# RMS normalisation of rows on one core: the first store on ScalarE's queue cut to one row, two stores and two loads of the first slot joined

## The chip, the cores and the metric

The kernel runs on one core of one Trainium2 chip. The metric is the device time of one execution in microseconds (us). All engine names are those of the profile: PE is TensorE, DVE is VectorE, ACT is ScalarE, POOL is GpSimd, SP is SyncE, which here only issues DMAs. ACT issues some DMAs too, on a queue of its own.

## The reference

```python
# x: 16 x 1024 x 512, float32; gamma: 512, float32
rms = np.sqrt(np.mean(x ** 2, axis=-1, keepdims=True) + 1e-5)
return (x / rms * gamma).astype(np.float32)
```

Each of the 16384 rows of 512 numbers is divided by its root mean square and multiplied by gamma. In and out are 33.55 MB each, and every byte is moved once.

## The kernel before

**Tiles and slots.** The rows are cut into 4 tiles (0 to 3). A tile has 128 partitions with 32 consecutive rows each, so 8.39 MB; "rows a to b" below means rows a to b of every partition, and in memory these are one run of 2 KB a row per partition. There are three slots (`slots`, line 40) of a tile's size in SBUF. Tiles 0, 1 and 2 live in slots 0, 1 and 2; tile 3 is loaded into slot 0 again, so its load has to wait until tile 0 is stored. Everything is done in place. An unwritten part of slot 2, its rows 23 to 31, serves as scratch for the squares of the groups with a piece of 9 rows (line 91), which is why these rows of tile 2 are loaded by themselves, later.

**Groups.** `groups` (line 76) lists the units of work in order: (tile, first row, rows, pieces, share of POOL). Tile 0 has three groups (rows 0-6, 7-15, 16-31), the others two each (rows 0-15, 16-31). For every group:

- `square_sums` (L96, L97): for each piece ACT squares the rows into PSUM, an SBUF scratch or slot 2, and DVE adds up each row.
- `inverse_rms` (L102, L103): ACT takes the root, DVE the reciprocal.
- `scale_by_pool` (L109, L110): POOL does the last 3, 5 or 7 rows of the group alone, first times 1/rms, then times gamma.
- `scale` (L118): ACT multiplies the other rows by 1/rms, one instruction a row.
- `times_gamma` (L122): DVE multiplies these rows by gamma, which lies in PSUM (PE spread it there at the start).

**Order.** The schedule is manual: each engine runs its instructions in the order of the program text. The loop from line 163 on is software-pipelined: while group k is scaled, the squares and sums of group k+1 are made. On ACT, the first two squares of group k+1 come ahead of the first half of the scaling of group k, and a third square ahead of the second half. So a square that waits for a load holds the scaling of the group before it.

**Transfers.** `load` (L45) goes on SP's queue, `store` (L49) on SP's or ACT's. A DMA instruction waits, on its issuing engine, for the semaphores of what it reads or overwrites; a reader of loaded rows waits for the semaphore of the DMA that brought them, which is full when the whole DMA has landed. SP's list, in order: tile 0 in four loads with gamma in between, tile 1 in two, tile 2 rows 0-22, then store tile 0 rows 8-15, store tile 0 rows 16-31, load tile 2 rows 23-31, load tile 3 rows 0-15, load tile 3 rows 16-31, store tile 1 rows 4-31, store tile 2, store tile 3 in two halves. ACT's list has three stores: tile 0 rows 0-3 (line 173, after the first squares of the group from row 16), tile 0 rows 4-7 (line 179) and tile 1 rows 0-3 (line 181).

Of the kernel before, what the change touches and what calls it, by code (L numbers as in the profile page):

```python
# [9 lines left out]
def kernel(  # L10
# [6 lines left out]
    nc = tc.nc  # L17
# [26 lines left out]
    def load(t, slot, r0, r1):  # L44
        dma = nc.sync.dma_start(out=slots[slot][:, r0:r1], in_=xv[t][:, r0:r1])  # L45
        before_scale.append((slot, r0, r1, dma))

    def store(t, slot, r0, r1, queue=nc.sync):
        dma = queue.dma_start(out=ov[t][:, r0:r1], in_=slots[slot][:, r0:r1])  # L49
        before_scale.append((slot, r0, r1, dma))  # L50
# [38 lines left out]
    def square_sums(ss, t, g, r, m, k):  # L89
        if m == 9:  # L90
            sq = slots[2][:, 23:32, :]
        else:
            home, name, most = ((psum, "sq_psum", 7), (const, "sq_sbuf", 5))[k % 2]
            sq = home.tile([P, most, D], fp32, name=name)
        rows = slots[slot_of[t]][:, g + r : g + r + m, :]
        nc.scalar.activation(out=sq[:, :m], in_=rows, func=AF.Square)  # L96
        nc.vector.tensor_reduce(  # L97
            out=ss[:, r : r + m, 0], in_=sq[:, :m], axis=mybir.AxisListType.X, op=OP.add
        )

    def inverse_rms(ss, n):
        nc.scalar.activation(out=ss[:, :n, 0], in_=ss[:, :n, 0], func=AF.Sqrt, bias=eps_t, scale=1.0 / D)  # L102
        nc.vector.reciprocal(out=ss[:, :n, 0], in_=ss[:, :n, 0])  # L103
        return ss

    def scale_by_pool(rstd, t, g, n, share):
        part = slots[slot_of[t]][:, g + n - share : g + n, :]
        by_row = rstd[:, n - share : n].to_broadcast([P, share, D])
        nc.gpsimd.tensor_tensor(out=part, in0=part, in1=by_row, op=OP.mult)  # L109
        last = nc.gpsimd.tensor_tensor(  # L110
            out=part, in0=part, in1=gamma_b.to_broadcast([P, share, D]), op=OP.mult
        )
        before_scale.append((slot_of[t], g + n - share, g + n, last))

    def scale(rstd, t, g, r0, r1):
        x = slots[slot_of[t]]
        for r in range(r0, r1):
            nc.scalar.activation(out=x[:, g + r, :], in_=x[:, g + r, :], func=AF.Copy, scale=rstd[:, r])  # L118

    def times_gamma(t, g, r0, r1):  # L120
        part = slots[slot_of[t]][:, g + r0 : g + r1, :]
        scaled = nc.vector.tensor_tensor(  # L122
            out=part, in0=part, in1=gamma_psum.to_broadcast([P, r1 - r0, D]), op=OP.mult
        )
        for slot, b0, b1, earlier in before_scale:
            if slot == slot_of[t] and b0 < g + r1 and g + r0 < b1:
                tc.declare_no_dep(scaled.ins, earlier.ins, reason="ScalarE waited for it before it scaled these rows")

    def transfers(t, g):
        if (t, g) == (0, 0):  # L130
            load(1, 1, 16, 32)
            load(2, 2, 0, 23)
        elif (t, g) == (0, 16):
            store(0, 0, 8, 16)
            store(0, 0, 16, 32)
            load(2, 2, 23, 32)
            load(3, 0, 0, 16)
            load(3, 0, 16, 32)
        elif (t, g) == (1, 16):
            store(1, 1, 4, 32)  # L140
        elif (t, g) == (2, 16):
            store(2, 2, 0, 32)
        elif (t, g) == (3, 0):
            store(3, 0, 0, 16)
        elif (t, g) == (3, 16):
            store(3, 0, 16, 32)

    def pieces_of(group):
        t, g, n, pieces, share = group
        ss = stats.tile([P, 16, 1], fp32, name="ss")  # L150
        r = 0
        todo = []
        for k, m in enumerate(pieces):
            todo.append((ss, t, g, r, m, k))
            r += m
        return ss, todo
# [6 lines left out]
    for k, group in enumerate(groups):  # L163
        t, g, n, pieces, share = group
        mine = n - share
        half = (mine + 1) // 2
        ahead = groups[k + 1 :][:1]
        ss, todo = pieces_of(ahead[0]) if ahead else (None, [])
        scale_by_pool(rstd, t, g, n, share)
        for piece in todo[:2]:  # L170
            square_sums(*piece)
        if (t, g) == (0, 7):
            store(0, 0, 0, 4, nc.scalar)
        scale(rstd, t, g, 0, half)
        for piece in todo[2:]:
            square_sums(*piece)
        scale(rstd, t, g, half, mine)
        if (t, g) == (0, 16):
            store(0, 0, 4, 8, nc.scalar)
        elif (t, g) == (2, 0):  # L180
            store(1, 1, 0, 4, nc.scalar)
        times_gamma(t, g, 0, mine)
        transfers(t, g)
        for nxt in ahead:
            rstd = inverse_rms(ss, nxt[2])
# [30 lines left out]
```

## Time and profile before

| what | value |
|---|---|
| median of 3 runs | 161.56 us (161.45 to 161.64) |
| the profiled execution's own time | 161.69 us |
| its span in the trace | 159.8 us |
| DVE busy | 112.0 us (70% of the span), 39 instructions |
| ACT busy | 107.8 us (67%), 108 instructions |
| POOL busy | 106.4 us (67%), 24 instructions |
| PE busy | 2.0 us (1%) |
| SP's queue (q1) | 63.97 MB, 93.5% of 16 DMA engines' span |
| ACT's queue (q10) | 3.15 MB, 4.7% |

Times within the execution are counted from the start of the span. The span is what the trace shows from first to last event; the execution's own time is 1.9 us longer. A landing is the moment at which a DMA's semaphore is full; each of the 16 DMA engines adds its part, and the trace records these 16 completions one by one. The trace also records each packet that a DMA engine moved, with its queue, start, length in bytes and duration; in this kernel a packet is one partition's run of rows, so each DMA of 128 partitions is 8 packets on each of 16 engines. A share of the queues above is the time that its packets took.

### The profile page before, as it was taken

The page shows a single profiled execution, that of the slowest core. Times are in us where ns is not written, and L with a number is a line of the kernel's source. Part 1 is how long each engine was busy: PE and PEld are TensorE (multiplying, and loading weights), DVE is VectorE, ACT ScalarE, POOL GpSimd, SP SyncE. Part 2 cuts the span into 40 slices and gives each one's busy share as a digit, 9 for nine tenths or more (in the row PEclk, how much of TensorE's full clock was granted, in tenths as well). Part 3 has the DMA queues.
Part 4 walks back from the last instruction along what each step waited for, and adds up shares of the span by engine and source line. Part 5 has one row for each costly group of instructions (what it writes and reads, how often), then busy time and mean ns, then how long its engine had stood idle before and what let it go on. Part 6 is the DMA issues. An engine that isn't in the chain of part 4 may idle for free.

```text
span 159.8 us, 273 instructions
## 1 busy us (share of the span) xinstructions
PE 2.0 (1%) x2; PEld 0.5 (0%) x2; DVE 112.0 (70%) x39; ACT 107.8 (67%) x108; POOL 106.4 (67%) x24
## 2 busy tenths in 40 slices
PE   0050000000000000000000000000000000000000
PEld 0010000000000000000000000000000000000000
DVE  0019098899798999999999999999999009800000
ACT  3071966975999999999899999989970990000000
POOL 1000960994999599999999999999999990000000
DMA  5999999999999998998999999999996997999995
GB/s 179 431 427 468 443 418 410 377 449 408 455 476 443 443 410 365 423 500 370 434 468 394 470 445 390 501 459 459 459 476 279 525 476 312 394 468 451 394 435 222
DMA packets 2747, 67.12 MB, mean 420 GB/s; under 512 B 313, under 2 KB 314, under 8 KB 442
## 3 DMA queue, kind: packets, MB, share of 16 engines
q1 hardware_dynamic: 2314, 63.97, 93.5%
q10 hardware_dynamic: 432, 3.15, 4.7%
q14 instruction: 1, 0.01, 0.0%
HBM read 33.56 MB, written 33.55 MB: 420 GB/s over the span
## 4 chain that ended last, share of the span: by engine, by line
DVE 59%; ACT 21%; DMA 4%; issue 1%; ACTq 1%; SPq 0%
DVE ss L97 36%; DVE slot L122 23%; ACT slot L118 8%; ACT slot L96 8%; ACT sq_psum L96 5%; DMA slot<-in_x_dram 4%; DVE ss L103 1%; ACT ss L102 0%; ACTq L211 0%; ACT gamma_b L162 0%; SPq L45 0%; ACTq L49 0%; ACTq L96 0%
## 5 line engine op out<-in xcount | busy, mean ns | idle before, releaser
L109 POOL TENSOR_TENSOR slot<-slot,ss 128x3584 f32<-128x3584 f32 (+2 forms) x9 | 46.9, 5213 | 24.2 <-DVE ss L103 24.2
L110 POOL TENSOR_TENSOR slot<-slot,gamma_b 128x3584 f32<-128x3584 f32 (+2 forms) x9 | 59.2, 6582 | 0.7
L97 DVE TENSOR_REDUCE ss<-sq_psum 128x7 f32<-128x3584 f32 (+1 forms) x13 | 42.2, 3245 | 13.7 <-ACT sq_psum L96 13.7
L118 ACT ACTIVATE slot<-slot,ss 128x512 f32<-128x512 f32 x75 | 47.2, 706 | 4.7 <-DVE ss L103 4.7
L122 DVE TENSOR_TENSOR slot<-slot,gamma_psum 128x4608 f32<-128x4608 f32 (+2 forms) x9 | 41.3, 4589 | 8.7 <-ACT slot L118 8.7
L96 ACT ACTIVATE sq_psum<-slot 128x3584 f32<-128x3584 f32 (+1 forms) x13 | 34.5, 2657 | 6.3 <-DMA slot<-in_x_dram 5.7
L97 DVE TENSOR_REDUCE ss<-slot 128x9 f32<-128x4608 f32 x3 | 14.9, 4954 | 4.4 <-ACT slot L96 4.2
L97 DVE TENSOR_REDUCE ss<-sq_sbuf 128x5 f32<-128x2560 f32 x5 | 14.0, 2800 | 0.0
L96 ACT ACTIVATE slot<-slot 128x4608 f32<-128x4608 f32 x3 | 12.1, 4032 | 0.0
L96 ACT ACTIVATE sq_sbuf<-slot 128x2560 f32<-128x2560 f32 x5 | 11.6, 2324 | 0.3 <-DMA slot<-in_x_dram 0.3
L102 ACT ACTIVATE ss<-ss,eps_t 128x16 f32<-128x16 f32 (+2 forms) x9 | 2.7, 304 | 11.7 <-DVE ss L97 11.7
L103 DVE RECIPROCAL ss<-ss 128x16 f32<-128x16 f32 (+2 forms) x9 | 2.1, 235 | 0.4 <-ACT ss L102 0.4
L66 PE MATMUL gamma_psum<-gamma_row,ones_col 1*128 1x512 f32 x2 | 2.0, 1122 | 8.7 <-DMA gamma_row<-in_gamma_dram 8.7
L72 ACT ACT_TABLE_LOAD x1 | 1.3, 1283 | 1.2 <-PEq L200 1.2
L162 ACT COPY gamma_b<-gamma_psum 128x512 f32<-128x512 f32 x1 | 0.6, 564 | 0.0
L66 PEld LDWEIGHTS gamma_psum<-gamma_row,ones_col 1*128 1x128 f32 x2 | 0.5, 305 | 8.6 <-issue 8.6
L64 POOL MEMSET ones_col<- 1x128 f32 x1 | 0.2, 194 | 0.3 <-POOLq L200 0.3
L200 POOL MEMSET const-float32-0.0<- 128x1 f32 x1 | 0.1, 98 | 0.2 <-issue 0.2
L72 ACT ACTIVATE table<-eps_t 128x1 f32<-128x1 f32 x1 | 0.2, 202 | 0.0
L200 POOL MEMSET const-bfloat16-1.0<- 128x1 bf16 x1 | 0.1, 101 | 0.0
L200 POOL MEMSET const-uint8-127<- 128x1 uint8 x1 | 0.1, 101 | 0.0
L200 POOL MEMSET const-float32-1.0<- 128x1 f32 x1 | 0.1, 98 | 0.0
(1 smaller groups left out, 0.1 us busy)
## 6 DMA issues: line engine op xcount, KB each, us to landing
slot<-in_x_dram SPq DMA_DIRECT2D x5, 4096.0 KB, 25.0
out_dram<-slot SPq DMA_DIRECT2D x3, 4096.0 KB, 20.2
out_dram<-slot SPq DMA_DIRECT2D x1, 7168.0 KB
slot<-in_x_dram SPq DMA_DIRECT2D x1, 5888.0 KB
out_dram<-slot ACTq DMA_DIRECT2D x3, 1024.0 KB
slot<-in_x_dram SPq DMA_DIRECT2D x1, 2304.0 KB, 25.7
slot<-in_x_dram SPq DMA_DIRECT2D x1, 2048.0 KB, 10.0
out_dram<-slot SPq DMA_DIRECT2D x1, 2048.0 KB
```

The costliest lines, as they stand in the source:

```text
L66: nc.tensor.matmul(gamma_psum[:, 0], ones_col, gamma_row, start=True, stop=True)
L72: nc.scalar.activation(out=table, in_=eps_t, func=AF.Sqrt)
L96: nc.scalar.activation(out=sq[:, :m], in_=rows, func=AF.Square)
L97: nc.vector.tensor_reduce(out=ss[:, r : r + m, 0], in_=sq[:, :m], axis=mybir.AxisListType.X, op=OP.add)
L102: nc.scalar.activation(out=ss[:, :n, 0], in_=ss[:, :n, 0], func=AF.Sqrt, bias=eps_t, scale=1.0 / D)
L103: nc.vector.reciprocal(out=ss[:, :n, 0], in_=ss[:, :n, 0])
L109: nc.gpsimd.tensor_tensor(out=part, in0=part, in1=by_row, op=OP.mult)
L110: last = nc.gpsimd.tensor_tensor(out=part, in0=part, in1=gamma_b.to_broadcast([P, share, D]), op=OP.mult)
L118: nc.scalar.activation(out=x[:, g + r, :], in_=x[:, g + r, :], func=AF.Copy, scale=rstd[:, r])
L122: scaled = nc.vector.tensor_tensor(out=part, in0=part, in1=gamma_psum.to_broadcast([P, r1 - r0, D]), op=OP.mult)
L162: nc.scalar.copy(out=gamma_b[:, 0], in_=gamma_psum[:, 0])
L200: nc = _bacc.Bacc("TRN2", target_bir_lowering=False, num_devices=1)
```

## The change

Row 0 of tile 0 goes out alone in the first store on ACT's queue, rows 1 to 7 in the second, where there were 0 to 3 and 4 to 7. Tile 0's rows 8 to 31 are stored by one DMA on SP's queue, at the place in the program where the second of two stood. Tile 3's 32 rows are loaded by one DMA in place of two.

In the instruction lists, SP's has one store and one load fewer; the order on all other engines is what it was. The semaphores of the later DMAs are dealt out anew, since the DMAs of the program take eight of them in turn.

```diff
         elif (t, g) == (0, 16):
-            store(0, 0, 8, 16)
-            store(0, 0, 16, 32)
+            store(0, 0, 8, 32)
             load(2, 2, 23, 32)
-            load(3, 0, 0, 16)
-            load(3, 0, 16, 32)
+            load(3, 0, 0, 32)
...
         if (t, g) == (0, 7):
-            store(0, 0, 0, 4, nc.scalar)
+            store(0, 0, 0, 1, nc.scalar)
         scale(rstd, t, g, 0, half)
...
         if (t, g) == (0, 16):
-            store(0, 0, 4, 8, nc.scalar)
+            store(0, 0, 1, 8, nc.scalar)
```

## Prediction

> **What bounds the kernel now.** I read the page's second part first, then the stretches, the DMA issues and the timelines of SP, ACT and DVE. Two rows of the page, the DMA engines' busy tenths in 40 slices of 4 us and the bytes:
>
> ```profile
> DMA  5999999999999998998999999999996997999995
> HBM read 33.56 MB, written 33.55 MB: 420 GB/s over the span
> ```
>
> No compute engine passes 70%, but the 16 DMA engines are full from the first slice to the last (a packet counts in the slice in which it starts, hence the 6 and 7 late on, where packets are long). The view by stretches gives the rate; the last columns are DMA share and GB/s:
>
> ```profile
> 0.70:1.70 1.00, 0.00 (x0) 0.00 (x0) 0.00 (x0) 0.53 (x1) 0.23 (x2) 1.00 0.00 0
> 1.70:2.00 0.30, 0.00 (x0) 0.00 (x0) 0.00 (x0) 0.30 (x1) 0.00 (x0) 1.00 0.94 109
> ...
> 28.00:32.00 4.00, 0.00 (x0) 0.00 (x0) 3.40 (x1) 4.00 (x2) 4.00 (x1) 1.00 0.95 354
> 32.00:81.30 49.30, 0.00 (x0) 0.00 (x0) 47.53 (x17) 45.13 (x45) 45.13 (x8) 1.00 1.01 436
> ...
> 139.60:149.30 9.70, 0.00 (x0) 0.00 (x0) 0.00 (x0) 0.00 (x0) 0.00 (x0) 1.00 1.00 432
> ```
>
> So some 433 GB/s, with no hole between transfers. The bytes do not change, so the time changes only if the queues run empty. The page's chain of waits names DVE (59%); that chain ends in a store that was issued early enough to queue, so DVE's slack counts, not its share. The issues of SP that set it (start, duration):
>
> ```profile
> 76.33 0.33 SPq L45 DMA_DIRECT2D slot<-in_x_dram  x1
> 111.67 0.34 SPq L49 DMA_DIRECT2D out_dram<-slot  x1
> 139.25 0.33 SPq L49 DMA_DIRECT2D out_dram<-slot  x1
> ```
>
> They are load(3, rows 16-31), store(2, all rows) and the last store, whose landing comes 19.7 us after issue (view of DMA issues), at 158.95. Back from there at 433 GB/s: 4.19 MB is 9.69 us, so store(3, 0-15) lands at 149.3, store(2) at 139.6, store(1, 4-31) at 120.2. **Slack** of the issue before the queue empties: 120.2 - 111.7 = 8.5 us for store(2), 13.9 for store(3, 0-15) (issued 125.65), 10.0 for the last. Packets end about 0.4 us before the landing is recorded (single packet records: 158.0 to 158.6 against 158.95), so the queue of store(1) is dry, as a mean over the engines, at 119.55 unless store(2) stands behind it.
>
> **Part 1: the ACT stores, one row and seven in place of four and four.** Both are issued where they were (27.41 and 40.02), on the same waits by the instruction lists: the first still follows DVE's product of rows 0-3. Bytes are equal, and SP's loads keep the engines full (436 GB/s from 32 on). Packets are one row-run per partition, so 2 and 14 KB in place of 8 and 8. The second must land before tile 3 may be loaded. Before, it took from 40.02 to 59.7 (recorded completions); seven rows in 8 rounds beside SP's 46 KB packets (433 GB/s are 27 an engine) take 8 x (1.74 + 0.53) = 18.2 us after a start near 44, landing near 62, long before 76. Cost 0. One thing is open: 28 to 32, around the first ACT store, moves 354 GB/s where 433 is usual, 0.32 MB or 0.7 us. If that is the price of this store's size, up to -0.7; if more, smaller packets cost, as much again. No other ACT store shows it; I take 0.
>
> **Part 2: store(0, 8-31) in one.** SP issued rows 8-15 at 39.78 and 16-31 at 55.45. Now all wait for DVE's product of rows 16-24 (ends 55.4) and go at 55.45. Ahead of them stands load(2, 0-22), recorded as landing at 61.5: 6 us of cover, some 5 after a start-up of about 1. Same bytes, same place in SP's queue: 0. Only with that cover gone would it cost.
>
> **Part 3: load(3) in one; here the price is.** Its issue waits for store(0, 8-31) to land (76.2, as the rows 16-31 did; load 3 of rows 16-31 went at 76.33) and has load(2, 23-31) ahead of it in the queue until 81.5: no hole. But rows 0-15 were issued at 66.45, landed 25.1 us later, at 91.55, and ACT squared them at once:
>
> ```profile
> 91.61 0.31 ACT L102 ACTIVATE ss<-ss,eps_t 128x16 f32<-128x16 f32 x1 [0.35 <-DVE ss L97]
> 91.82 3.14 ACT L96 ACTIVATE sq_psum<-slot 128x3584 f32<-128x3584 f32 x1
> 94.90 2.32 ACT L96 ACTIVATE sq_sbuf<-slot 128x2560 f32<-128x2560 f32 x1
> 97.13 3.15 ACT L118 ACTIVATE slot<-slot,ss 128x512 f32<-128x512 f32 x5
> 100.37 1.88 ACT L96 ACTIVATE sq_psum<-slot 128x2048 f32<-128x2048 f32 x1
> 102.19 2.54 ACT L118 ACTIVATE slot<-slot,ss 128x512 f32<-128x512 f32 x4
> ```
>
> Now one semaphore covers all 32 rows (in the instruction list the square at 91.82 waits for this DMA, the one of rows 16-31 for none). Behind it on ACT's queue stand the nine row scalings (L118) of tile 2's second half, and DVE's product and store(2) wait for those.
>
> When does it land? Rows 16-31 landed at 103.4 (last recorded completion), after the whole 1.05 MB of the ACT store of tile 1 (issued 86.70). That store's 8 KB packets (0.31 us) go in between SP's, nearly one for one, the first 3.65 us after issue, three of SP's 32 KB packets (1.21 us) later. SP's packets are now 64 KB and take 2.42 us (those of store(2), same size, do), so fewer ACT packets get ahead of the load's eight. It starts at 81.1; packets end at 83.5, 85.9, 88.4, 90.8, 93.2...; ACT's enter at 90.8 or 93.2, and 4 or 3 of 8 are in before the eighth. So 103.4 less 4 or 5 times 0.31: **102.0**. Bounds: all ahead 103.4; none ahead 100.9.
>
> By the Trainium skill (DMA: Bandwidth & Descriptors, Queues, rings and completion order) an engine drains a whole packet of some 9 to 17 descriptors from one row before it switches, so the eight pieces would go together. The trace shows them one by one here; by the page the bound of 103.4 would hold and the time be near 164.6.
>
> From there: ACT starts 0.08 us after a landing (81.53 to 81.61 at tile 2's last rows), so 102.1, not 91.82. DVE's rows of before:
>
> ```profile
> 96.52 3.82 DVE L97 TENSOR_REDUCE ss<-sq_psum 128x7 f32<-128x3584 f32 x1
> 100.26 2.80 DVE L97 TENSOR_REDUCE ss<-sq_sbuf 128x5 f32<-128x2560 f32 x1
> 102.98 2.28 DVE L97 TENSOR_REDUCE ss<-sq_psum 128x4 f32<-128x2048 f32 x1
> 105.18 4.94 DVE L122 TENSOR_TENSOR slot<-slot,gamma_psum 128x4608 f32<-128x4608 f32 x1
> ```
>
> Before, DVE was the later one; now ACT is. ACT by its own starts: 3.1 + 2.2 + 3.2 + 1.8 + 2.5 = 12.8 us to the end of the last scaling (DVE's first reduction, of 7 rows, ends 7.0 after the start, before ACT's third square needs its tile at 8.5), so the product starts at 114.9, ends at 119.85, and store(2) is issued at 119.9 (POOL's part is done at 111.65). A start on an idle queue: first load issued at 0.74, nothing moves until 1.7, 0.94 busy after it, some 1.1 us to the mean first packet. On a busy queue 3.65 (above) was measured. I take 1.1, because the queue is empty: packets from 121.0. **Gap 121.0 - 119.55 = 1.45 us.**
>
> By the Trainium skill (DMA: Bandwidth & Descriptors, Specifications) the first byte on this path takes about 0.6 us; by it the gap would be 0.95. No row here restarts a store on an empty queue.
>
> What is late next: tile 3's halves. DVE is full again, so from product to product 13.69 us as before (105.18 to 118.87), and 15.38 from there to the last product's end: 119.85 + 13.7 + 15.4 = 148.95, issue at 149.0, packets from 150.1. The queue before it empties at 121.0 + 19.4 + 9.7 = 150.1. So the last store is just at the edge: 0 to 0.4, I take 0.15.
>
> **Sum**: 0 + 0 + 1.45 + 0.15 = +1.6 us. The profiled execution took 161.69 (span 159.8, 1.9 around it), so 163.3; it lies 0.13 above the median 161.56, and that gives **163.2 us**.
>
> **Rivals.**
> - *Later landing*: all ACT packets go ahead of the load, 103.4, gap 1.4 larger: 164.6. Against: the one-for-one mix.
> - *Slow restart*: an empty queue needs the 3.65 us of the busy one, so 2.55 more: 165.7. For: it is measured on a store; against: there packets stood ahead.
> - *Not slower, hidden*: the load goes ahead of ACT's packets altogether. Landing at 100.9, store(2) at 118.8, packets at 119.9: gap 0.35, time 161.9; it decides at a landing of 100.85, where 0.3 us is left: just beyond that bound, or at it with a restart quicker by 0.05. For: long packets are favoured; against: ACT's are due three of the load's packets before its end.
> - *Faster*: fewer, larger transfers pay, and the last rows come in time. Of the transfers' borders none shows a hole (432 GB/s over 139.6 to 149.3); only the 0.7 us at 28 to 32 could be won: 160.9 without a gap. The Trainium skill (DMA: Bandwidth & Descriptors, Rules for kernel authors) advises to coalesce into one large transfer, which speaks for this change; the trace shows no cost between queued ones.
> - The change does do what it says: SP's list has one store and one load fewer, the other engines' orders are unchanged.
>
> **Chances.** Forecast (landing 101.6 to 102.4, restart 1.0 to 1.6, edge 0 to 0.4, so +1.0 to +2.6) 0.68; later landing 0.10; slow restart 0.09; hidden or nearly 0.08, of which 0.05 within 0.2% (0.32 us, about what a measurement of this kernel can tell from none); faster 0.05. Faster 0.05, same 0.05, slower 0.90. The range 162.0 to 165.0 holds the forecast, the later landing and part of the nearly hidden.
>
> **What would show it.** The DMA row: a hole near 120 us, and not before. ACT idle from 91.9 to 102, DVE from 96.5 to 105.3. store(2) issued at 119.9 in place of 111.7, the last at 149.0. ACT's second store landing near 62, load(3) issued at 76. If load(3) is issued later, or a hole shows near 60 or 80, parts 1 or 2 are wrong; if the hole is 3 us and more, the restart or the landing is.

## The result, and the profile after

The changed kernel takes 163.79 us (median of 6 runs, 163.24 to 164.93), the kernel before 161.60 (161.45 to 161.71): a ratio of 1.0145, with a 95% interval of 1.0116 to 1.0175. That is 2.2 us more, where 1.6 was forecast. The profiled execution is the longest of the six: 164.93 us, span 163.1. So its profile shows about 1 us more than the median, and the experiments below are needed to say which part of its loss is steady.

The same two rows of the page as before, busy tenths of the DMA engines and bytes:

```profile
DMA  6999899999989998897997989999919959889885
HBM read 33.56 MB, written 33.55 MB: 411 GB/s over the span
```

The bytes are the same, the rate over the span is 411 GB/s in place of 420, and one slice, the thirtieth (118.3 to 122.4 us), holds a 1 where the others hold 5 to 9. Seen closely, in the view by stretches (the last two columns are DMA share and GB/s; a packet counts in the stretch in which it starts):

```profile
116.00:118.00 2.00, 0.00 (x0) 0.00 (x0) 1.80 (x2) 2.00 (x4) 0.00 (x0) 1.00 1.06 459
118.00:120.00 2.00, 0.00 (x0) 0.00 (x0) 2.00 (x1) 2.00 (x1) 0.00 (x0) 1.00 0.27 115
120.00:122.00 2.00, 0.00 (x0) 0.00 (x0) 2.00 (x3) 2.00 (x2) 0.00 (x0) 1.00 0.00 0
122.00:124.00 2.00, 0.00 (x0) 0.00 (x0) 2.00 (x2) 2.00 (x4) 1.87 (x1) 1.00 1.23 524
```

No packet starts between 120 and 122. ACT and DVE are busy there and POOL is idle: the queue waits for computed rows. ACT's timeline names the cause; the bracket is the idle time before an instruction and what ended it:

```profile
92.03 0.29 ACT L102 ACTIVATE ss<-ss,eps_t 128x16 f32<-128x16 f32 x1
104.16 3.16 ACT L96 ACTIVATE sq_psum<-slot 128x3584 f32<-128x3584 f32 x1 [11.84 <-DMA slot<-in_x_dram]
107.26 2.32 ACT L96 ACTIVATE sq_sbuf<-slot 128x2560 f32<-128x2560 f32 x1
109.48 3.17 ACT L118 ACTIVATE slot<-slot,ss 128x512 f32<-128x512 f32 x5
112.56 1.86 ACT L96 ACTIVATE sq_psum<-slot 128x2048 f32<-128x2048 f32 x1
114.36 2.55 ACT L118 ACTIVATE slot<-slot,ss 128x512 f32<-128x512 f32 x4
```

ACT stands 11.84 us before the square of tile 3's first rows, for their load. The scalings of tile 2 (L118, from 109.48) stand behind it, though their rows had landed by 82.4 and DVE had made their 1/rms by 97.3. Then DVE's product, and SP's store of tile 2, which went at 111.67 before; the third line is the last store:

```profile
116.94 4.95 DVE L122 TENSOR_TENSOR slot<-slot,gamma_psum 128x4608 f32<-128x4608 f32 x1 [0.20 <-ACT slot L118]
```

```profile
76.58 0.33 SPq L45 DMA_DIRECT2D slot<-in_x_dram  x1
121.96 0.34 SPq L49 DMA_DIRECT2D out_dram<-slot  x1
151.06 0.33 SPq L49 DMA_DIRECT2D out_dram<-slot  x1
```

By the records of single packets, store(1)'s last packets ended between 119.51 and 121.62, as a mean at 120.2, and store(2)'s first started between 122.80 and 122.95, 0.9 us after the issue. So the engines stood idle for 2.7 us on average. In the kernel before, store(1)'s last packets ended at 119.6 as a mean: another 0.6 us had been lost ahead of the hole.

One thing was not forecast. The load's sixteen completions lie at 101.84 to 102.59 for twelve DMA engines, around the 102.0 of the prediction, and at 103.84 to 104.14 for four. ACT waits for the last.

### The profile page after: what moved, and what is told of

Its sections match the earlier page's. It is cut to its first block, busy times and chain, and to the rows that moved or that the text cites. A ratio compares the mean times of both kernels' runs of the same rounds, so it can differ in the third digit from the quotient of the medians.

```text
span 163.1 us, 270 instructions
## 1 busy us (share of the span) xinstructions
PE 2.0 (1%) x2; PEld 0.5 (0%) x2; DVE 112.6 (69%) x39; ACT 107.7 (66%) x108; POOL 106.3 (65%) x24
## 4 chain that ended last, share of the span: by engine, by line
DMA 34%; DVE 27%; ACT 27%; issue 3%; ACTq 1%; SPq 0%
DMA slot<-in_x_dram 21%; DVE ss L97 14%; DVE slot L122 13%; DMA out_dram<-slot 13%; ACT slot L118 11%; ACT slot L96 7%; ACT sq_psum L96 6%; ACT sq_sbuf L96 1%; ACT ss L102 0%; ACTq L209 0%; ACT gamma_b L160 0%; SPq L45 0%; ACTq L49 0%; DVE ss L103 0%; SPq L49 0%
## 5 line engine op out<-in xcount | busy, mean ns | idle before, releaser
L118 ACT ACTIVATE slot<-slot,ss 128x512 f32<-128x512 f32 x75 | 47.4, 708 | 4.7 <-DVE ss L103 4.7
```

## The experiments

They ran on two chips, each beside runs of the kernel before, whose medians lie at 161.59 to 161.65. The second run of ACT's stores, the two runs that cut its seven rows and the last run are from one chip, all others from another. Theory A is that of the prediction: the load in one lands as a whole, ACT's queue stands, store(2) comes after its queue is dry. The rivals: the new transfer sizes make DMA engines lag (B), or the loss is in parts 1 or 2 (C).

**The load in one, alone.**

```diff
-            load(3, 0, 0, 16)
-            load(3, 0, 16, 32)
+            load(3, 0, 0, 32)
```

> Only tile 3 is loaded in one; the four stores of tile 0 are as before. Theory A (the one load lands as a whole, ACT's square of tile 3's first half waits for it, holds tile 2's scaling, and the queue runs dry near 120 us): all of the loss is here, 163.2 to 163.8 us, store(2) issued near 120 or later. Theory B (the new sizes, 2, 14 and 48 KB packets, make DMA engines lag behind the others, and that is the larger part): less than half of the loss, below 162.6. Theory C (the loss is in parts 1 or 2, the load's price is hidden): 161.6.

Measured: 163.01 us (162.89 to 163.32), ratio 1.0086 (1.0067 to 1.0105), so 1.4 us. Its SP issues of store(2) and of the last store:

```profile
120.01 0.34 SPq L49 DMA_DIRECT2D out_dram<-slot  x1
149.09 0.33 SPq L49 DMA_DIRECT2D out_dram<-slot  x1
```

and its stretches around the hole:

```profile
117.00:118.80 1.80, 0.00 (x0) 0.00 (x0) 1.80 (x1) 1.80 (x2) 0.00 (x0) 1.00 1.18 510
118.80:119.20 0.40, 0.00 (x0) 0.00 (x0) 0.40 (x1) 0.40 (x1) 0.00 (x0) 1.00 0.00 0
119.20:120.60 1.40, 0.00 (x0) 0.00 (x0) 1.40 (x3) 1.40 (x2) 0.43 (x1) 1.00 0.01 0
120.60:121.20 0.60, 0.00 (x0) 0.00 (x0) 0.60 (x1) 0.60 (x2) 0.60 (x1) 1.00 4.09 1748
```

Here the load landed at 101.68 to 102.20 on all engines, store(2) was issued at 120.01 (forecast 119.9) and the last store at 149.09 (149.0). The queue was dry at 119.40 as a mean, store(2)'s first packets started at 120.90: a hole of 1.5 us. All runs lie within 0.45 us. So the steady part of the loss is theory A's, and it comes from this load. But it is 1.4 us, not 2.2, and 163.01 lies below the 163.2 to 163.8 that theory A gave for all of the loss.

**The stores alone** (parts 1 and 2, tile 3 loaded in two).

```diff
-            load(3, 0, 0, 32)
+            load(3, 0, 0, 16)
+            load(3, 0, 16, 32)
```

> The changed kernel with tile 3 loaded in two again, so parts 1 and 2 alone (stores of 1, 7 and 24 rows). Theory A: 161.6 us like the kernel before, with store(2) issued near 111.7; engines that lag cost nothing, since 8 us of queued work stand ahead. Theory B: 162.3 or more, with some engines' packets ending later than the others'. Theory C: 163 or more.

Measured: 161.99 us, but from 161.50 to 163.36 over 12 runs; ratio 1.0038 (1.0013 to 1.0063). The profiled execution (161.56) has no hole and issues store(2) at 111.59. So the stores cost nothing in some executions and up to 1.8 us in others. The median missed both theory A's 161.6 and theory B's 162.3 or more. Something adds to A's loss in part of the executions; that it is a lag cannot be seen here, since the profiled execution is a quick one. The next two experiments tell which store it is.

**ACT's stores of 1 and 7 rows, alone.**

```diff
-            store(0, 0, 0, 4, nc.scalar)
+            store(0, 0, 0, 1, nc.scalar)
...
-            store(0, 0, 4, 8, nc.scalar)
+            store(0, 0, 1, 8, nc.scalar)
```

> Only the two stores on ACT's queue are changed (1 and 7 rows); the store of rows 8-31 and the load of tile 3 stay in two. Stores of 1, 7 and 24 rows together gave 161.5 to 163.4 us, median 162.0, so some executions lose up to 1.8 us. If the 2 and 14 KB packets of these two stores make engines lag, this kernel shows the same spread, median 161.8 to 162.1. If it is the joined store (48 KB packets, some of which took 2.3 to 2.9 us in place of 1.8), this one is like the kernel before: 161.6, no run over 162.0.

Measured: 163.21 us (161.63 to 163.84), ratio 1.0077 (1.0049 to 1.0106). Nine of 12 runs are over 162.5 us, and the median is over the 161.8 to 162.1 expected for a loss that lies in these stores.

**The store of rows 8-31 in one, alone.**

```diff
-            store(0, 0, 8, 16)
-            store(0, 0, 16, 32)
+            store(0, 0, 8, 32)
```

> Only the store of tile 0's rows 8-31 is joined; ACT's stores are 4 and 4 rows, tile 3 is loaded in two. If the joined store's long packets make engines lag: median 161.8 to 162.1 with runs up to 163. If the 2 and 14 KB packets do: 161.6, no run over 162.0.

Measured: 161.67 us (161.54 to 163.14), ratio 1.0012 (0.9995 to 1.0030): no difference that can be measured, one of 12 runs over 162.5.

**ACT's stores alone, a second time.**

> The same kernel as the earlier one with only ACT's stores of 1 and 7 rows, which took 161.6 to 163.8 us with a median of 163.2, while its profiled execution was one of the quick ones (161.66). If the loss belongs to these stores: again most executions at 162.5 to 163.8; a profile of a long one would show a few of the 16 DMA engines' completions 1 to 2 us behind the rest from some point on, to the end. If it was a disturbance of that hour: 161.6.

Measured: 161.76 us (161.51 to 163.87), ratio 1.0040 (1.0006 to 1.0075); five of 12 runs over 162.5, where most were expected. So the loss comes again, on another chip, in part of the executions only, and the share varies (9 and 5 of 12). Over the three runs with these stores and the old loads, 18 of 36 executions are over 162.5; of the kernel before, beside all the experiments, 4 of 83. The profiled execution was again one without the loss (161.76), so none of this kernel shows where it arises.

**Seven rows as three and four.** At the second place, the first store staying at one row:

```diff
-            store(0, 0, 1, 8, nc.scalar)
+            store(0, 0, 1, 4, nc.scalar)
+            store(0, 0, 4, 8, nc.scalar)
```

> Row 0 alone in ACT's first store; at the place of the second, rows 1-3 and rows 4-7 as two stores (6 and 8 KB packets in place of 14 KB). If the 14 KB packets are the cause: 161.6 to 161.8. If it is that more of ACT's bytes come late, after 41 us, or that the first store's packets are only 2 KB: 162.5 or more, as with 7 rows in one.

Measured: 161.90 us (161.63 to 162.40), ratio 1.0015 (1.0003 to 1.0028).

**Rows 1 to 3 early again**, as a store of their own:

```diff
             store(0, 0, 0, 1, nc.scalar)
+            store(0, 0, 1, 4, nc.scalar)
...
-            store(0, 0, 1, 8, nc.scalar)
+            store(0, 0, 4, 8, nc.scalar)
```

> Rows 0 and 1-3 as two stores at the first place, rows 4-7 at the second: 2 KB packets first, no 14 KB packets, and the bytes as early as in the kernel before. If the 2 KB packets of the first store are the cause: 162.5 or more. If the late bytes or the 14 KB packets are: 161.6 to 161.8.

Measured: 161.95 us (161.78 to 162.56), ratio 1.0019 (1.0004 to 1.0034). With the 14 KB packets gone in either way, the times over 162.6 are gone too, also where the first store has one row and the other seven go late. Over 162.5 there is none of 12 in the first of the two and three of 12 in the second (162.53 to 162.56). Both medians lie 0.1 to 0.15 us over the 161.6 to 161.8 expected. That speaks for the 14 KB packets, or one DMA of seven rows, and against the single row and the later bytes.

The records of single packets show where the lag comes up in the two profiles that have it, the changed kernel's and that of the cut at row 28 below. When the seven-row store begins, most engines take its first packet at 43.6 to 44.2 us. A few take one more packet of SP's load first and come to it at 45.5 to 46.0: four engines in the changed kernel, two in the cut. From there each engine can be followed, since a packet starts where the one before it ended. All six lead to the slow packets at the end of the joined store, which started at 73.3 to 73.7 and took 2.3 to 2.9 us in place of 1.8 (for some of the six a neighbouring packet fits the path as well). From there on as many engines are late. In the four other profiles with a seven-row store (the two with ACT's stores alone, the stores alone, and tile 2 scaled first) all 16 engines take the first packet at 43.6 to 44.3, and none lags. So in all six profiles the lag goes with a late turn at the seven-row store. That the turn is the cause is not shown, nor why a late turn at 44 us should make a packet at 73 slow.

**Cut at row 28**, first with all else as in the changed kernel:

```diff
-            load(3, 0, 0, 32)
+            load(3, 0, 0, 28)
+            load(3, 0, 28, 32)
```

> The changed kernel with tile 3 loaded as rows 0-27 and 28-31. Theory A: the square needs rows 0-15 only and waits for 28 rows, so it starts 2.4 us earlier than with 32 (28 rows are 16.96 us of the queue in place of 19.37), near 99.5 to 101.5; store(2) is issued near 117.5 to 119.5, at the edge of the queue's end less the restart of 0.9 us: 161.6 to 162.3. Theory B or C (sizes, or the number of transfers): as the changed kernel, 163.2 and more.

Measured: 163.03 us (161.81 to 163.31), ratio 1.0074 (1.0048 to 1.0100): a miss. In the profiled execution the first part's completions spread from 99.25 to 101.31, the last one counts, and store(2) went at 119.12: its first packets started at 119.96 to 120.11 on 14 engines whose store(1) had ended at 119.5 to 120.0, a hole of 0.3 us as a mean. Most of the loss is two late engines: the last store's completions lie at 159.16 to 159.31 on 14 engines and at 160.20 to 160.28 on two (before, all within 0.55 us). An engine that fell behind stays behind here, since every DMA gives each engine the same bytes.

The same cut with the stores of the kernel before:

> The load of tile 3 alone is changed, and cut at row 28 (rows 0-27, 28-31), with the stores of the kernel before. By theory A the first part lands near 99.1, store(2) is issued near 117.0, its packets could start at 117.9 (restart 0.9 us), 1.6 before the queue is dry: 161.6 us. If the price hung on the size of the transfer or on what a second transfer brings, it would stay near the 163.0 of the one load.

Measured: 161.96 us (161.58 to 162.23), ratio 1.0015 (1.0005 to 1.0025). Its wait for the load and its issue of store(2):

```profile
100.20 3.16 ACT L96 ACTIVATE sq_psum<-slot 128x3584 f32<-128x3584 f32 x1 [8.36 <-DMA slot<-in_x_dram]
```

```profile
117.98 0.34 SPq L49 DMA_DIRECT2D out_dram<-slot  x1
```

ACT still stands for 8.4 us, and it costs nothing: with 0.9 us of restart the packets could start at 118.9, before the queue is dry. The 0.3 us that remains is not a hole; 16 of the load's 56 KB packets took some 0.5 us longer between 96 and 100 us.

**Tile 2 scaled first.** With the load in one, the nine scalings and the product of tile 2's second half are put ahead of tile 3's squares:

```diff
+        first = (t, g) == (2, 16)
+        if first:
+            scale(rstd, t, g, 0, mine)
+            times_gamma(t, g, 0, mine)
         for piece in todo[:2]:
             square_sums(*piece)
...
-        scale(rstd, t, g, 0, half)
+        if not first:
+            scale(rstd, t, g, 0, half)
```

(the later `scale` and `times_gamma` likewise).

> The changed kernel, still with one load of 32 rows, but for the second half of tile 2 the nine scalings and the product with gamma stand ahead of the squares and sums of tile 3 on ACT and DVE. Theory A: what waits for the load no longer holds store(2), which goes at 111.7 when POOL is done; the first square of tile 3 still waits for the load (near 102 to 104), the last store is issued near 146 with some 2 us to spare, and no hole is left: 161.6 us. If the order costs DVE more than worked out here, up to 163. Theory B: 163 and more, as the transfers are those of the changed kernel.

Measured: 163.32 us (163.15 to 164.25), ratio 1.0116 (1.0090 to 1.0143), another miss, and an instructive one. Its three last issues on SP, and its stretches:

```profile
111.42 0.34 SPq L49 DMA_DIRECT2D out_dram<-slot  x1
...
133.76 0.33 SPq L49 DMA_DIRECT2D out_dram<-slot  x1
...
149.17 0.33 SPq L49 DMA_DIRECT2D out_dram<-slot  x1
```

```profile
118.00:122.00 4.00, 0.00 (x0) 0.00 (x0) 2.84 (x1) 4.00 (x4) 4.00 (x1) 1.00 1.10 475
147.00:149.00 2.00, 0.00 (x0) 0.00 (x0) 2.00 (x1) 0.00 (x0) 0.00 (x0) 1.00 0.57 246
149.00:151.00 2.00, 0.00 (x0) 0.00 (x0) 0.09 (x1) 0.00 (x0) 0.00 (x0) 1.00 0.61 262
```

Store(2) goes at 111.42 and the hole at 120 is gone, as theory A says. But ACT and DVE now take turns at tile 3 instead of overlapping (ACT waits twice for DVE there, some 3 us each), the last store goes at 149.17 in place of the 146 worked out, and a new hole stands at 148.6 to 150.0. To take this one away as well, POOL gets five rows of the last group in place of three (stores of tile 0 as before):

```diff
-        (3, 16, 16, (7, 5, 4), 3),
+        (3, 16, 16, (7, 5, 4), 5),
```

> Tile 3 loaded in one, the stores as before; tile 2's second half is scaled and multiplied by gamma ahead of tile 3's squares, and POOL does 5 rows of the last group in place of 3, so ACT has 11 and DVE 11. The version with 3 had no hole at 120 us but one at 148.5 to 150.3, since its last store went at 149.2. With 5 the last product ends 2.2 us earlier, the issue is near 146.9, packets 147.8, and the queue is dry at 148.3: no hole at all, 161.6 us. If the load in one costs by itself, 162.5 and more.

Measured: 161.80 us (161.57 to 162.03), ratio 1.0008 (1.0000 to 1.0017). Its last product and last issue:

```profile
140.85 6.02 DVE L122 TENSOR_TENSOR slot<-slot,gamma_psum 128x5632 f32<-128x5632 f32 x1 [6.91 <-ACT slot L118]
```

```profile
146.95 0.33 SPq L49 DMA_DIRECT2D out_dram<-slot  x1
```

With the whole load in one DMA and both holes closed, the loss is gone. It does not beat the kernel before: the bytes are the same, and there is no hole in either.

**Both joined, ACT's stores as before.**

```diff
-            store(0, 0, 8, 16)
-            store(0, 0, 16, 32)
+            store(0, 0, 8, 32)
...
-            load(3, 0, 0, 16)
-            load(3, 0, 16, 32)
+            load(3, 0, 0, 32)
```

> The changed kernel with ACT's stores of 4 and 4 rows again: the store of rows 8-31 and the load of tile 3 joined. The load in one alone gave 163.0 (162.9 to 163.3), the joined store alone 161.7. If the two are all of the steady price and ACT's stores make the rest: 163.0, within 162.8 to 163.4. If the changed kernel's spread (163.2 to 164.9) comes of the joined store and the late landing together: 163.6 to 164 with runs over 164.

Measured: 163.19 us (162.97 to 164.16), ratio 1.0099 (1.0075 to 1.0122): five of six runs within 162.97 to 163.39. The remaining 0.6 us to the changed kernel's 163.79 is then, by difference, the part of ACT's two stores; the two intervals of the ratios just overlap, so its size is not settled.

## Why the prediction was right, point by point

- **The number.** Of the 2.2 us, 1.4 are the hole that was forecast as 1.45. The other 0.6 to 0.8 us are ACT's two stores, by difference; the profile shows lagging engines, for which the prediction had no term. That the time still lies in the range is luck for this part.
- **The bound.** Right: the bytes did not change, and without a hole and without a lag the loss is gone. The load in one with both holes closed gave 161.8, the load cut at row 28, with the old stores, 162.0.
- **Part 3.** Right within 0.2 us where no engine lags. Landing 102.0, in the load-alone kernel 101.7 to 102.2. ACT's packets go one by one between the load's 64 KB packets: by 101 us, just before the load's last packets end, 63 of the 128 had started, four an engine, where the prediction had 3 or 4 of 8 from the old trace. Store(2) 119.9 against 120.01; hole 1.45 against 1.5; last store 149.0 against 149.09. That the hole fits to 0.05 is luck in part: the issue came 0.1 later, the restart was 0.2 shorter, and the queue was dry 0.15 earlier (119.40). The edge term of 0.15 was nothing: the last store's packets started when those before them ended.
- **The restart.** 1.1 us taken from the start of the kernel, 0.9 measured on the stores. The slow restart of 3.65 us falls: that figure belongs to a queue with packets ahead. The Trainium skill (DMA: Bandwidth & Descriptors, Specifications) gives about 0.6 us to the first byte. The traces have 0.84 to 0.99 from the start of the issue, which is what the sum needs, and the measurement decides; from the end of the issue, 0.34 us later, they have 0.50 to 0.65.
- **Later landing.** By the Trainium skill (the same page, Queues, rings and completion order), as the prediction reads it, ACT's eight packets an engine would have gone together and the load come at 103.4. In the load-alone kernel they did not. The changed kernel's last four engines did come at 103.8 to 104.1, but because they lagged: by 101 us no more of ACT's packets had started there (63 of 128) than in the load-alone kernel.
- **Part 2.** Right: the joined store alone is not told apart from the kernel before.
- **Part 1** is the term that was mis-sized: costed at 0, with "up to -0.7; if more, smaller packets cost, as much again" left open. Over the three runs with these stores and the old loads, half of the executions lose some 1 to 2.2 us; the medians are 0.1 to 1.6 us over the kernel before, the ratios 1.0038 to 1.0077. The bigger packets of the second store are the suspects, not the small ones of the first. The 0.7 us at 28 to 32 us was not won. It was over-sized, too, since the view counts a packet's bytes where the packet starts. With each packet's bytes spread over its own time, the kernel before moves 382 GB/s there, a loss of 0.5 us. The changed kernel moves 432 there, but 413 at 42 to 52 beside the seven-row store, where the kernel before has 432. The prediction asked whether these stores land in time, and they do (61.0 to 63.2, forecast 62); it did not ask whether an engine that loses time is late for everything after.
- **Not slower** and **faster** fall: no engine completed the load in one before 101.7, and joining paid nowhere (the joined store alone: 0.9995 to 1.0030). The advice of the Trainium skill to coalesce that the prediction quotes (DMA: Bandwidth & Descriptors, Rules for kernel authors) stands there for many small transfers; those joined here are of 2 and 4 MB.

What stays open is why some of the 16 engines fall behind, and that in some executions only. No profile of the kernels that hold the seven-row store with the old loads caught an execution with the loss, so that a lag makes it there is argued, not shown. The two lagging profiles (the changed kernel, the cut at 28) hold the joined store too, and its last packets are where engines fall behind: four in the changed kernel, 0.5 to 1.1 us over their usual 1.8, and two in the cut, 0.9 and 1.0 over. The two profiles that have the joined store without the seven-row store show no such packet.

## What to carry to other kernels

A DMA's reader waits for all of it: before two loads are joined, ask which engine's queue the first rows' reader heads, and what stands behind it. When the transfers are the bound, a wait of an engine costs nothing until its store misses the end of the queue: count each store's issue against that end (8.4 us of ACT's wait were free here, 10.5 cost 1.4), and after a repair look for the next store that is late. A reader waits for the last of the 16 engines. Slack in the queue does not cover an engine that lags: in the cut at row 28 the two late engines had no hole after store(1), and still ended the program 1 us after the others.

## What the runs showed of the hardware that was not expected

- DMA engines drift apart. In the changed kernel's profile four of 16, slow first at 73 to 76 us, completed the load 1.3 us and more after the other twelve, and store(1) still with the same distance; only the hole at 120 brought them together again (store(2)'s completions lie within 0.2 us).
- ACT's stores beside SP's loads go with a dip of the rate. With each packet's bytes spread over its own time, 28 to 32 us moves 382 to 388 GB/s in all six profiles whose first store has four rows, and 429 to 432 in the six with one row first and seven later. These six have their dip at 42 to 52 instead: 413 to 423, where the others have 432 or 433. Why is not shown.
